# Eight PSUM banks in one ring and an earlier fourth product in the seven-product stage of a two-layer encoder

## The chip, the cores and the metric

One core of one Trainium2 chip. The metric is device time in microseconds (us) of one launch, as the median of several runs. The profile is one more execution, recorded instruction by instruction.

## The reference

Two layers, 1152 tokens (1024 of a prompt, 8 x 16 of a sample), model width 1024, feed-forward width 4096, all in float32:

```python
h = rms_norm(x, g1); q, k, v, a, b = split(h @ w_in)
x = x + concat([attention(q, k, v) * beta_a, conv(a * sigmoid(b)) * beta_c]) @ w_out
h = rms_norm(x, g2)
x = x + square(relu(h @ w_up)) @ w_down
```

The last line, the feed-forward, is what the change is about.

## The kernel before, in words

Tokens lie in three blocks of 384 (`BT`), transposed, so that x of a block is eight tiles of 128 x 384. Every float32 number is split into a high and a low part (`parted` for activations: a cast on ACT, L807, and a subtraction on DVE, L808; for weights a cast on ACT, L884, and a subtraction on POOL, L885), and a product of a 128x128 weight tile and a 128x384 activation tile is three matmuls (high by high, high by low, low by high).

The feed-forward of blocks 0 and 1 runs in part as a *stage of seven products*: block 0 and block 1, and four quarters of a weight block, are treated as a 2x2 by 2x2 block product and multiplied in seven products in place of eight. This stage takes the last half of the hidden columns, in four groups in each layer. A group is two *ups* (`pair_up`, j = 0 and 1, each seven products of 12 matmuls, L918) and one *down* (`pair_down`, two halves `mp`, each seven products into two banks of six matmuls, L992): 336 matmuls. `quad` loads the four quarters of a weight block by four DMAs (raw and A tiles); the call `sums()` inside it makes S1, S2, S3 (L871 on DVE, 128x512), and the product with S4 makes S4. An up leaves eight forms of the hidden activations (B11, T1, T2, B22, T3, B21, T4) as high and low parts in the tiles F; the down adds each finished bank to x (L995, DVE). In the down, `then` (a generator, `second()` in `run`) brings the third block's x back from memory (`kept`) and computes its RMSNorm, in pieces between products of the last group.

A compile-time scheduler sets the order on each engine from the code, the pools and its own estimate of durations; a tile that is allocated from a pool waits until the readers of the bank's last holder are done. PSUM has eight banks: three in pool `pp` (tag g, `pg()`) and five in `px` (tag x, `px_bank()`). Before, an up's three accumulators A, B, Z are three g banks, the five "less" and "plus" results stand in x banks, a down's four accumulators X and Z in x banks, and its product A12·B21 in a g bank for each half.

The RMSNorm lines named below: L235 and L247 are the small statistics (POOL, PE), L241 a PE sum over the squares (L260, ACT), L275 the product with the scale.

Of the kernel before, what the change touches and what calls it, by code (L numbers as in the profile page):

```python
# [10 lines left out]
AF = mybir.ActivationFunctionType  # L11
# [50 lines left out]
class Kernel:  # L62
# [628 lines left out]
    def hidden(self, ps):  # L691

        nc = self.nc
        hid = self.hp.tile([128, 2, BT], F32R, tag="hid", name=self.nm("hid"), bufs=4)
        f = self.tmp()
        nc.scalar.activation(f, ps, AF.Relu)  # L696
        nc.scalar.activation(f, f, AF.Square)
        nc.scalar.copy(hid[:, 0], f)  # L698
        nc.vector.tensor_tensor(out=hid[:, 1], in0=f, in1=hid[:, 0].bitcast(F32), op=ALU.subtract)  # L699
        return hid  # L700
# [204 lines left out]
            self.ahead = self.quad(src)  # L905
        return form, (lambda: self.ahead("sums")) if src is not None else (lambda: None)

    def pair_up(self, H, F):

        nc = self.nc  # L910
        form, sums = self.next_quad()
        A, B, Z = (self.pg()[0] for _ in range(3))

        def product(w, h, ps, start):
            u = form(w)
            for k in range(4):
                for i, (p, q) in enumerate(((0, 0), (0, 1), (1, 0))):
                    nc.tensor.matmul(ps, lhsT=u[:, p, k], rhs=H[h](q, k), start=start and k == 0 and i == 0, stop=k == 3 and i == 2, skip_group_check=True)  # L918

        def copy(ps):  # L920
            t = self.tmp()
            nc.scalar.copy(t, ps)
            return t

        def plus(o, t, ps):
            nc.vector.tensor_tensor(out=o, in0=t, in1=ps, op=ALU.add)
            return o

        def hidden(n, src, t):
            nc.scalar.activation(t, src, AF.Relu)  # L930
            nc.scalar.activation(t, t, AF.Square)
            return split(n, t)

        def split(n, t):
            self.parted(t, lambda p: F(n)[:, p])
            return t

        def less(n, x, y):
            t = self.px_bank()
            nc.vector.tensor_tensor(out=t, in0=x, in1=y, op=ALU.subtract)  # L940
            return split(n, t)

        product("A11", "B11", A, True)
        c1 = copy(A)
        product("S1", "T1", Z, True)
        z5 = copy(Z)
        product("S2", "T2", A, False)
        u2 = copy(A)
        product("S4", "B22", Z, False)
        b12 = plus(self.px_bank(), u2, Z)  # L950
        nc.scalar.activation(b12, b12, AF.Relu)
        nc.scalar.activation(b12, b12, AF.Square)
        product("S3", "T3", A, False)
        b22 = plus(z5, z5, A)
        b22 = hidden("B22", b22, b22)
        sums()
        product("A12", "B21", B, True)
        less("T3", b22, b12)
        b11 = plus(c1, c1, B)
        b11 = hidden("B11", b11, b11)  # L960
        product("A22", "T4", A, False)
        t1 = less("T1", b12, b11)
        t2 = less("T2", b22, t1)
        b21 = hidden("B21", A, self.tmp())
        less("T4", b21, t2)

    def px_bank(self):
        return self.px.tile([128, 512], F32, tag="x", name=self.nm("x"), bufs=5)[:, :BT]
# [8 lines left out]
    def pair_down(self, F, xs, between):  # L977

        nc = self.nc
        for mp in range(2):  # L980
            form, sums = self.next_quad()
            X, Z = ([self.px_bank() for _ in range(2)] for _ in range(2))
            for wn, hn, ps, start, b, half in (("A11", "B11", X, True, 0, 0), ("S1", "T1", Z, True, 1, 1), ("S2", "T2", X, False, 1, 0),
                                               ("S4", "B22", Z, False, 1, 0), ("S3", "T3", X, False, 1, 1), ("A12", "B21", None, True, 0, 0),
                                               ("A22", "T4", X, False, 0, 1)):
                u = form(wn)
                for i in range(2):
                    o = self.pg()[0] if ps is None else ps[i]
                    n = 0
                    for j in range(2):  # L990
                        for p, q in ((0, 0), (0, 1), (1, 0)):
                            nc.tensor.matmul(o, lhsT=u[:, p, 2 * i + j], rhs=F(j, hn)[:, q], start=start and n == 0, stop=n == 5, skip_group_check=True)  # L992
                            n += 1
                    m = 4 * half + 2 * mp + i
                    nc.vector.tensor_tensor(out=xs[b][:, m], in0=xs[b][:, m], in1=o, op=ALU.add)  # L995
                if wn == "S3":
                    sums()
                if between is not None:
                    next(between, None)

    def pair_feed(self, l, groups, xs, forms, then):
        for g in groups[::2]:
            F = self.hidden_forms()
            for j in range(2):
                self.pair_up(forms, lambda n, j=j: F(j, n))
            self.pair_down(F, xs, then if g == groups[-2] else None)

    def run(self):
        nc, tc, a = self.nc, self.tc, self.a
# [7 lines left out]
        x = [self.load_x(src[0])]  # L1017
# [3 lines left out]
        for l in range(DEPTH):  # L1021
            self.u, self.co, self.k, self.vb = [None] * NB, [None] * NB, [], []
            x, h, ao = [None] * NB, [None] * NB, [None] * NB
# [60 lines left out]
            forms, three, fourth = self.pair_forms(h[0], h[1])  # L1084
# [16 lines left out]
            def second(x=x, h=h, l=l):  # L1101
                x[2] = self.load_x(kept, self.mark)
                self.arena = [self.slot([4, 2, BT], F32, "f"), 0]
                for i, h[2] in enumerate(self.rmsnorm_steps(x[2], l, G2)):
                    for _ in range((5, 3, 1)[i]):
                        yield
                self.arena = None

# [1 line left out]
            self.aux = None  # L1110
            with pool(name=f"xp{l}", bufs=1) as self.xp, pool(name=f"px{l}", bufs=1, space=PS) as self.px:
                self.ahead("sums")
                then = second()
                self.pair_feed(l, range(pair, NG), x, forms, then)
                for _ in then:
                    pass
# [137 lines left out]
```

## Time and profile before

| | |
|---|---|
| median of 3 runs | 2439.61 us (2438.41 to 2440.89) |
| profiled execution | 2441.61 us, its span 2439.8 us |
| mean granted TensorE clock | 0.984 |
| PE busy | 2333.8 us (96%) |
| DVE, POOL, ACT busy | 1633.8 (67%), 1529.2 (63%), 1270.2 us (52%) |
| DMA | mean 109 GB/s |

PE is TensorE's matmuls, DVE VectorE, ACT ScalarE, POOL GpSimd. PE is busy nearly all the time, so the question of this kernel is where PE waits, and where it runs at a lower clock.

### The profile page before, as it was taken

What the parts mean: (1) busy time and instruction counts of PE and PEld (TensorE: products, weight loads), DVE (VectorE), ACT (ScalarE), POOL (GpSimd) and SP (SyncE); (2) the same over time, 40 slices, a digit from 0 to 9 for tenths busy, and PEclk for the clock granted to TensorE, in tenths of its full rate; (3) what the DMA queues carried; (4) which work ended last, traced back from release to release, by engine and by line L of the source; (5) the groups of instructions that cost most, each with busy time, mean ns of one, the idle gap of its engine ahead of it and who ended that gap; (6) DMA issues with size and microseconds to landing.
All of it is one profiled execution on the core that took longest, in us unless ns stands there. A gap on an engine that the chain in (4) does not pass through costs nothing.

```text
span 2439.8 us, 39000 instructions
## 1 busy us (share of the span) xinstructions
PE 2333.8 (96%) x13822; PEld 2268.8 (93%) x13822; DVE 1633.8 (67%) x2993; ACT 1270.2 (52%) x2732; POOL 1529.2 (63%) x1375
## 2 busy tenths in 40 slices
PE   6898899999998999999999999999999899999999
PEld 6888898989998998999999999999999899999999
DVE  4999986996376767687687764699834766752222
ACT  5467555654335555554566476466433554544442
POOL 6875575556466566776865776856445655666663
PEclk9999899999999999999999999999999999999999
DMA  5422433334322222444343344434333222245442
GB/s 177 138 90 91 120 104 109 111 102 134 113 91 70 70 70 70 163 122 129 103 121 107 118 155 131 130 98 126 96 106 102 61 65 70 83 146 148 126 128 75
DMA packets 164259, 266.49 MB, mean 109 GB/s; under 512 B 24752, under 2 KB 55728, under 8 KB 164016
## 3 DMA queue, kind: packets, MB, share of 16 engines
q1 hardware_dynamic: 164064, 264.01, 34.9%
q8 instruction: 108, 1.77, 0.3%
q14 instruction: 87, 0.71, 0.1%
HBM read 250.19 MB, written 16.05 MB: 109 GB/s over the span
## 4 chain that ended last, share of the span: by engine, by line
PE 75%; DVE 14%; POOL 3%; ACT 3%; issue 2%; DMA 1%; SPq 0%; DVEq 0%; POOLq 0%; ACTq 0%
PE g L715 13%; PE g L213 13%; PE g L215 13%; PE g L214 13%; PE x L992 8%; DVE c L347 5%; PE g L918 4%; PE m L715 2%; PE r L715 2%; POOL w L885 2%; PE c L715 1%; PE g L992 1%; PE s L525 1%; DMA A<-in_w 1%; PE m L560 1%
## 5 line engine op out<-in xcount | busy, mean ns | idle before, releaser
L206 POOL TENSOR_TENSOR w<-raw,w 128x512 fp32r<-128x512 f32 x728 | 967.0, 1338 | 587.4 <-ACT w L205 567.8
L205 ACT CAST w<-raw 128x512 fp32r<-128x512 f32 x728 | 445.9, 619 | 459.2 <-PE g L715 126.1
L213 PE MATMUL g<-h,w 128*128 128x384 f32 x1696 | 576.6, 341 | 8.4 <-ACT h L276 3.8
L215 PE MATMUL g<-h,w 128*128 128x384 f32 x1696 | 573.5, 338 | 0.0
L214 PE MATMUL g<-h,w 128*128 128x384 f32 x1696 | 573.2, 338 | 0.0
L347 DVE SCALAR_TENSOR_TENSOR c<-u,vec,c 128x384 f32<-128x384 f32 (+1 forms) x960 | 498.1, 519 | 19.0
L715 PE MATMUL g<-hid,w 128*128 128x384 f32 x2304 | 430.5, 340 | 10.7 <-DVE x L717 7.3
L715 PEld LDWEIGHTS g<-hid,w 128*128 128x128 f32 x2304 | 398.4, 188 | 19.7 <-DVE x L717 12.1
L213 PEld LDWEIGHTS g<-h,w 128*128 128x128 f32 x1696 | 320.9, 189 | 12.6 <-ACT h L276 4.6
L214 PEld LDWEIGHTS g<-h,w 128*128 128x128 f32 x1696 | 320.9, 189 | 1.1 <-DVE h L277 0.2
L215 PEld LDWEIGHTS g<-h,w 128*128 128x128 f32 x1696 | 320.8, 189 | 0.7
L699 DVE TENSOR_TENSOR hid<-t,hid 128x384 fp32r<-128x384 f32 x128 | 108.8, 850 | 192.3 <-ACT hid L698 192.1
L885 POOL TENSOR_TENSOR w<-S,w 128x512 fp32r<-128x512 f32 x96 | 134.3, 1405 | 155.6 <-ACT w L884 154.6
L992 PE MATMUL x<-F,w 128*128 128x384 f32 x960 | 188.3, 350 | 0.0
L717 DVE TENSOR_TENSOR x<-x,g 128x384 f32<-128x384 f32 x240 | 129.5, 548 | 77.4 <-PE g L715 76.9
L992 PEld LDWEIGHTS x<-F,w 128*128 128x128 f32 x960 | 179.6, 199 | 0.0
L995 DVE TENSOR_TENSOR x<-x,x 128x384 f32<-128x384 f32 x192 | 102.7, 549 | 83.5 <-PE x L992 83.4
L918 PE MATMUL g<-h,w 128*128 128x384 f32 x768 | 147.3, 338 | 11.7 <-ACT t L930 9.0
L918 PEld LDWEIGHTS g<-h,w 128*128 128x128 f32 x768 | 134.0, 188 | 16.3 <-ACT t L930 11.5
L696 ACT ACTIVATE t<-g 128x384 f32<-128x384 f32 x128 | 62.9, 492 | 141.0 <-PE g L215 140.0
L884 ACT CAST w<-S 128x512 fp32r<-128x512 f32 x96 | 59.7, 625 | 109.4 <-PE x L992 71.5
L885 POOL TENSOR_TENSOR w<-raw,w 128x512 fp32r<-128x512 f32 x64 | 84.1, 1315 | 46.0 <-ACT w L884 46.0
(213 smaller groups left out, 3786.7 us busy)
## 6 DMA issues: line engine op xcount, KB each, us to landing
raw<-in_w SPq DMA_DIRECT2D x792, 256.0 KB, 2.7
A<-in_w SPq DMA_DIRECT2D x64, 256.0 KB, 2.7
x<-in_x SPq DMA_DIRECT2D x24, 384.0 KB, 5.0
x<-xd SPq DMA_DIRECT2D x12, 384.0 KB, 5.4
kept<-x SPq DMA_DIRECT2D x4, 768.0 KB, 4.6
x<-kept SPq DMA_DIRECT2D x8, 384.0 KB, 4.1
xd<-x SPq DMA_DIRECT2D x4, 768.0 KB, 4.2
out_y<-x SPq DMA_DIRECT2D x4, 768.0 KB, 4.3
```

The source lines that it names most:

```text
L205: nc.scalar.copy(u[:, 0], raw)
L206: nc.gpsimd.tensor_tensor(out=u[:, 1], in0=raw, in1=u[:, 0].bitcast(F32), op=ALU.subtract)
L213: nc.tensor.matmul(ps, lhsT=u(0, k), rhs=h(0, k), start=k == 0, stop=False)
L214: nc.tensor.matmul(ps, lhsT=u(0, k), rhs=h(1, k), start=False, stop=False)
L215: self.pe = nc.tensor.matmul(ps, lhsT=u(1, k), rhs=h(0, k), start=False, stop=k == KT - 1)
L347: t = nc.vector.scalar_tensor_tensor(out=o, in0=src(k), scalar=w, in1=o, op0=ALU.mult, op1=ALU.add)
L699: nc.vector.tensor_tensor(out=hid[:, 1], in0=f, in1=hid[:, 0].bitcast(F32), op=ALU.subtract)
L715: self.pe = nc.tensor.matmul(ps, lhsT=u(p), rhs=hid[:, q], start=i == 0, stop=i == n - 1)
L717: nc.vector.tensor_tensor(out=x[:, m], in0=x[:, m], in1=ps, op=ALU.add)
L885: nc.gpsimd.tensor_tensor(out=u[:, 1], in0=f[n], in1=u[:, 0].bitcast(F32), op=ALU.subtract)
L918: nc.tensor.matmul(ps, lhsT=u[:, p, k], rhs=H[h](q, k), start=start and k == 0 and i == 0, stop=k == 3 and i == 2, skip_group_check=True)
L992: nc.tensor.matmul(o, lhsT=u[:, p, 2 * i + j], rhs=F(j, hn)[:, q], start=start and n == 0, stop=n == 5, skip_group_check=True)
```

## The change

All banks of the stage come from one ring, `bank8()`, of eight turns: five from `px`, three from `pg`. The seventh and eighth bank of an up are saved by forming T3 in the bank of b12 and T4 in that of t1. In the up, A12·B21 moves from sixth to fourth product, with b11 made behind it, and S4·B22 from fourth to sixth. In the down, A12·B21 takes its two banks (`Y`) from the ring. The third block's reload starts (`next(then)`) in the last up in place of the last down.

```diff
-    def pair_up(self, H, F):
+    def pair_up(self, H, F, then=None):
...
-        A, B, Z = (self.pg()[0] for _ in range(3))
+        A, Z, B = (self.bank8() for _ in range(3))
...
-        def less(n, x, y):
-            t = self.px_bank()
+        def less(t, x, y):
             nc.vector.tensor_tensor(out=t, in0=x, in1=y, op=ALU.subtract)
-            return split(n, t)
+            return t
...
         u2 = copy(A)
-        product("S4", "B22", Z, False)
-        b12 = plus(self.px_bank(), u2, Z)
-        nc.scalar.activation(b12, b12, AF.Relu)
-        nc.scalar.activation(b12, b12, AF.Square)
+        product("A12", "B21", B, True)
+        if then is not None:
+            next(then)
+        b11 = plus(c1, c1, B)
+        b11 = hidden("B11", b11, b11)
         product("S3", "T3", A, False)
         b22 = plus(z5, z5, A)
         b22 = hidden("B22", b22, b22)
         sums()
-        product("A12", "B21", B, True)
-        less("T3", b22, b12)
-        b11 = plus(c1, c1, B)
-        b11 = hidden("B11", b11, b11)
+        product("S4", "B22", Z, False)
+        b12 = plus(self.bank8(), u2, Z)
+        nc.scalar.activation(b12, b12, AF.Relu)
+        nc.scalar.activation(b12, b12, AF.Square)
         product("A22", "T4", A, False)
-        t1 = less("T1", b12, b11)
-        t2 = less("T2", b22, t1)
+        t1 = split("T1", less(self.bank8(), b12, b11))
+        t2 = split("T2", less(self.bank8(), b22, t1))
+        split("T3", less(b12, b22, b12))
         b21 = hidden("B21", A, self.tmp())
-        less("T4", b21, t2)
+        split("T4", less(t1, b21, t2))
+
+    def bank8(self):
+
+        self.turn = (self.turn + 1) % 8
+        return self.px_bank() if self.turn < 5 else self.pg()[0]
...
-            X, Z = ([self.px_bank() for _ in range(2)] for _ in range(2))
+            X, Z, Y = ([self.bank8() for _ in range(2)] for _ in range(3))
...
-                    o = self.pg()[0] if ps is None else ps[i]
+                    o = ps[i]
...
-                self.pair_up(forms, lambda n, j=j: F(j, n))
+                self.pair_up(forms, lambda n, j=j: F(j, n), then if j and g == groups[-2] else None)
...
-                    for _ in range((5, 3, 1)[i]):
+                    for _ in range((3, 3, 1)[i]):
```

The number of instructions on each engine stays what it was. In the rows that follow, g_ and x_ are PSUM banks, F_ tiles of hidden forms, T_ and h_ forms of the stage's input, w_ weight forms, S_, raw_ and A_ weight quarters and their sums, t_ temporaries, x_2764 and x_4025 the two blocks of x.

**The join, on PE** (second group of layer 0, between the last product of its second up and the first half of its down). Before:

```order
L992 MATMUL g_8934<-F_8491,w_8923 128x384 x3
L918 MATMUL g_8665<-T_7166,w_8788 128x384 x12
L992 MATMUL g_8926<-F_8491,w_8923 128x384
L992 MATMUL g_8934<-F_8491,w_8923 128x384
L992 MATMUL x_8828<-F_8489,w_8832 128x384 x6
L992 MATMUL x_8829<-F_8489,w_8832 128x384 x6
```

Now:

```order
L918 MATMUL g_8659<-T_7166,w_8778 128x384 x12
L998 MATMUL g_8822<-F_8485,w_8843 128x384
L998 MATMUL g_8821<-F_8486,w_8860 128x384 x3
L998 MATMUL g_8822<-F_8485,w_8843 128x384 x2
L998 MATMUL x_8820<-F_8485,w_8826 128x384 x6
L998 MATMUL x_8824<-F_8487,w_8917 128x384 x3
L998 MATMUL g_8821<-F_8486,w_8860 128x384
L998 MATMUL g_8823<-F_8485,w_8843 128x384 x6
L998 MATMUL g_8821<-F_8486,w_8860 128x384 x2
L998 MATMUL g_8822<-F_8486,w_8878 128x384 x6
L998 MATMUL x_8824<-F_8487,w_8917 128x384
L998 MATMUL x_8825<-F_8487,w_8917 128x384 x4
```

The L918 row with w_8788 (now w_8778) is A22·T4, after which B21's second half is formed. Before, the down's product with B21 (F_8491) followed at once; now 30 matmuls stand between, and B21's second half is first read by the single matmul into x_8824 (F_8487 holds T3 and B21). After these twelve rows comes the second half's first bank, x_8959, which takes over bank x_8797.

**The join, on DVE** (same place). Before:

```order
L940 TENSOR_TENSOR x_8807<-t_8700,x_8803 128x384
L871 TENSOR_TENSOR S_9057<-raw_8963,A_8965 128x512
L808 TENSOR_TENSOR F_8491<-t_8811,F_8491 128x384
L871 TENSOR_TENSOR S_9059<-S_9057,raw_8959 128x512
L871 TENSOR_TENSOR raw_8963<-raw_8959,raw_8963 128x512
L808 TENSOR_TENSOR F_8490<-x_8807,F_8490 128x384
L940 TENSOR_TENSOR x_8816<-t_8811,x_8807 128x384
L995 TENSOR_TENSOR x_2764<-x_2764,x_8828 128x384
```

Now:

```order
L808 TENSOR_TENSOR F_8486<-x_8797,F_8486 128x384
L871 TENSOR_TENSOR S_9051<-raw_8955,A_8957 128x512
L1001 TENSOR_TENSOR x_4025<-x_4025,g_8822 128x384
L808 TENSOR_TENSOR F_8487<-x_8774,F_8487 128x384
L871 TENSOR_TENSOR S_9053<-S_9051,raw_8951 128x512
L871 TENSOR_TENSOR raw_8955<-raw_8951,raw_8955 128x512
L939 TENSOR_TENSOR x_8793<-t_8804,x_8797 128x384
L1001 TENSOR_TENSOR x_2764<-x_2764,x_8820 128x384
L808 TENSOR_TENSOR F_8487<-t_8804,F_8487 128x384
```

The L939 row is T4's subtraction, the last reader of bank x_8797 (T2); before, T4's subtraction (x_8816) freed no bank that the down waited for. In both orders the three sums of the next weight block (L871) stand ahead of it.

**The start of the stage, on PE** (layer 0). Before:

```order
L715 MATMUL g_7848<-hid_7405,w_7574 128x384 x3
L715 MATMUL g_7848<-hid_7490,w_7584 128x384 x3
L918 MATMUL g_7893<-h_3248,w_7896 128x384
L918 MATMUL g_7893<-h_3249,w_7896 128x384
...
L918 MATMUL g_7893<-h_3248,w_7896 128x384
L918 MATMUL g_7895<-T_7164,w_7913 128x384 x2
```

Now:

```order
L918 MATMUL x_7893<-h_3249,w_7896 128x384
L715 MATMUL g_7840<-hid_7405,w_7574 128x384 x3
L715 MATMUL g_7840<-hid_7490,w_7584 128x384 x3
L715 MATMUL g_7848<-hid_7405,w_7574 128x384 x3
L715 MATMUL g_7848<-hid_7490,w_7584 128x384 x3
L918 MATMUL x_7893<-h_3248,w_7896 128x384
L918 MATMUL x_7894<-T_7164,w_7913 128x384 x2
```

A11·B11 (w_7896) stood behind the last products of the stage ahead (L715); now 11 of its 12 matmuls stand before the last two of these, and S1·T1 (w_7913) follows them after one matmul. In layer 1 the order here is as it was.

## Rows read from the trace of the kernel before

**Rows 1.** The chain that ended last: shares of the span by engine.

```profile
PE 75%; DVE 14%; POOL 3%; ACT 3%; issue 2%; DMA 1%; SPq 0%; DVEq 0%; POOLq 0%; ACTq 0%
```

**Rows 2.** Stretches: length, busy PE, PEld, DVE, ACT, POOL (instructions), clock, DMA share, GB/s.

```profile
722.20:990.00 267.80, 246.64 (x1348) 239.92 (x1347) 186.76 (x303) 135.24 (x266) 159.13 (x119) 0.97 0.23 71
1900.10:2171.80 271.70, 251.95 (x1375) 245.21 (x1375) 188.98 (x306) 136.75 (x269) 161.13 (x122) 0.97 0.24 74
...
2160.00:2200.00 40.00, 40.00 (x231) 40.00 (x231) 11.82 (x19) 20.07 (x36) 29.66 (x23) 1.00 0.68 218
```

**Rows 3.** Waits of PE, whole run: us in total, times, longest.

```profile
PE g L992 <- ACT F L807: 17.8, 8, 3.0
...
PE g L918 <- ACT t L930: 9.0, 8, 1.1
...
PE g L241 <- DVE f L265: 2.5, 2, 1.3
...
PE g L992 <- ACT hid L807: 2.1, 2, 1.7
PE g L992 <- POOL w L885: 2.0, 2, 1.1
PE g L247 <- POOL s L235: 2.0, 2, 1.1
...
PE g L992 <- DVE x L926: 0.8, 2, 0.4
```

**Rows 4.** PE's timeline at a join: start, length, what, [idle before <-releaser].

```profile
824.26 2.35 PE L918 MATMUL g<-T,w 128*128 128x384 f32 x12
829.04 0.61 PE L992 MATMUL g<-F,w 128*128 128x384 f32 x2 [2.43 <-ACT F L807]
```

**Rows 5.** ACT's timeline at the same join.

```profile
826.65 0.49 ACT L930 ACTIVATE t<-g 128x384 f32<-128x384 f32 x1 [0.21 <-PE g L918]
...
828.48 0.51 ACT L807 CAST F<-t 128x384 fp32r<-128x384 f32 x1
```

**Rows 6.** Stretches after waits: one at full clock, the first of seven slow.

```profile
829.00:836.00 7.00, 6.96 (x40) 6.96 (x41) 7.00 (x13) 2.72 (x5) 3.37 (x4) 1.00 0.13 40
...
763.60:769.40 5.80, 5.80 (x20) 5.80 (x20) 5.35 (x11) 1.58 (x3) 0.64 (x1) 0.51 0.13 47
...
sum 31.20, PE 29.17 PEld 28.16 DVE 29.88 ACT 8.15 POOL 5.61; mean PE 4.17 PEld 4.02 DVE 4.27 ACT 1.16 POOL 0.80
```

**Rows 7.** DVE's timeline at the start of the stage, layer 0.

```profile
722.38 0.55 DVE L717 TENSOR_TENSOR x<-x,g 128x384 f32<-128x384 f32 x1 [0.48 <-PE g L715]
722.85 0.68 DVE L871 TENSOR_TENSOR S<-raw,A 128x512 f32<-128x512 f32 x1
...
724.78 1.77 DVE L871 TENSOR_TENSOR S<-raw,A 128x512 f32<-128x512 f32 x1
```

**Rows 8.** POOL at the same place, its timeline.

```profile
725.96 1.75 POOL L885 TENSOR_TENSOR w<-A,w 128x512 fp32r<-128x512 f32 x1
```

**Rows 9.** DVE's sums from 722 to 2172 by form, and DVE's waits there.

```profile
L871 DVE TENSOR_TENSOR S<-raw,A 128x512 f32<-128x512 f32 x32 | 30.6, 956 | 21.8 <-DMA A<-in_w 19.5 <-POOL w L885 1.7 <-issue 0.4
...
DVE S L871 <- DMA A<-in_w: 19.5, 15, 5.0
```

**Rows 10.** ACT in the last group of layer 0, its timeline.

```profile
951.69 0.85 ACT L260 ACTIVATE f<-x 128x768 f32<-128x768 f32 x1 [0.35 <-DMA x<-kept]
```

**Rows 11.** PE's timeline at the last product of an up.

```profile
886.57 0.69 PE L992 MATMUL g<-F,w 128*128 128x384 f32 x3
887.38 2.35 PE L918 MATMUL g<-T,w 128*128 128x384 f32 x12
```

**Rows 12.** The page's group of POOL's splits, and PE waiting for one at 726.

```profile
L885 POOL TENSOR_TENSOR w<-raw,w 128x512 fp32r<-128x512 f32 x64 | 84.1, 1315 | 46.0 <-ACT w L884 46.0
...
726.05 2.38 PE L918 MATMUL g<-T,w 128*128 128x384 f32 x12 [0.62 <-POOL w L885]
```

**Rows 13.** DVE where the third block's RMSNorm ends, its timeline.

```profile
960.35 4.29 DVE L275 SCALAR_TENSOR_TENSOR f<-x,vec,g 128x384 f32<-128x384 f32 x8 [0.21 <-PE g L247]
```

More of the change, by code (lines that the diff above doesn't have):

```diff
@@ L981, in pair_down @@
             form, sums = self.next_quad()
-            X, Z = ([self.px_bank() for _ in range(2)] for _ in range(2))
+            X, Z, Y = ([self.bank8() for _ in range(2)] for _ in range(3))
             for wn, hn, ps, start, b, half in (("A11", "B11", X, True, 0, 0), ("S1", "T1", Z, True, 1, 1), ("S2", "T2", X, False, 1, 0),
-                                               ("S4", "B22", Z, False, 1, 0), ("S3", "T3", X, False, 1, 1), ("A12", "B21", None, True, 0, 0),
+                                               ("S4", "B22", Z, False, 1, 0), ("S3", "T3", X, False, 1, 1), ("A12", "B21", Y, True, 0, 0),
                                                ("A22", "T4", X, False, 0, 1)):
@@ L1112, in run @@
                 self.ahead("sums")
+                self.turn = 7
                 then = second()
```

## The prediction

> **What bounds the kernel now.** I began with the chain that ended last: PE holds 75% of it and DVE 14% [rows 1], so time is won where PE waits or runs slowly. Next came the windows of the two stages that the change touches. They last 267.8 and 271.7 us, 539.5 together, and hold 1348 + 1375 = 2723 matmuls [rows 2]. A stretch without waits has 231 in 40 us [rows 2], 0.1732 us each. At that rate the stages would take 471.6 us; 68 are lost.
>
> The list of PE's waits shows where. The longest group is the *join*, where the first half of a down meets the end of its second up: PE waits for the cast of B21's second half (`L992 <- ACT F L807`), 17.8 us in eight waits, one in each of the eight groups; then 9.0 us in eight waits of the second up for the first up's last product to be read, since both use the same g bank [rows 3]. In the timeline 12 matmuls of A22·T4 start at 824.26 and are fed by 824.26 + 12 x 0.173 = 826.34; the next starts at 829.04 [rows 4]. That is 2.70 us where the list says 2.43, so a wait costs some 0.27 more than its idle time. ACT shows why: the relu starts at 826.65, and after a square the cast starts at 828.48 [rows 5].
>
> [...]
>
> **What the change removes.**
> (i) The wait for the first up's A, 9.0 us in eight: the second up's fourth product now has a ring bank that was free long before.
> (ii) The join's waits for B21 and its kin: 17.8 in eight, `ACT hid` 2.1 in two, `DVE x L926` 0.8 in two [rows 3]. The order now puts 30 matmuls, 5.2 us, between A22·T4 and the first use of B21's second half. The path to it takes 829.04 - 826.34 = 2.7 us [rows 4, 5]; 2.5 are to spare.
> (iii) `L241 <- DVE f` 2.5 and `L247 <- POOL s` 2.0, four waits in the reload's RMSNorm [rows 3]: by the new order some 50 matmuls, 8.7 us, stand between L241 and L247, and no wait was longer than 1.3.
> (iv) `L992 <- POOL w` 2.0 in two: same join, same cover [rows 3].
> Together 9.0 + 20.7 + 4.5 + 2.0 = 36.2 us in 26 waits; with 26 x 0.27 = 7.0 it is 43.2. Nearly all the falls of the clock stood behind these waits, so I give back 13 of the 15 us: 56.2. Bounds for that: 0 if waits as long as before return elsewhere, 15.
>
> **What it adds.** None of the following is a wait that the trace has at that place, so each is bounded by rows.
> *n1, start of layer 0.* S1 is summed on DVE behind the last x adds, which follow the last L715 products; 11 matmuls of A11·B11 that stood behind these as cover now stand before them. What is uncovered is at least that sum, 0.68 [rows 7], and at most the cover that went, 11 x 0.173 = 1.9; a cast follows the sum, so I take 1.9, once.
> *n2, the first ups.* POOL must make four splits while PE does 22 to 24 matmuls (3.8 to 4.2 us). A split takes 1.315 in the mean, four 5.3 [rows 12]: 1.0 late, twice. PE waited 0.62 for one here before [rows 12]. And b22's sum stands behind three L871 sums, 0.68 each alone and 1.77 at worst [rows 7]; 1.8 twice. Sum 5.6, bounds 2 and 8.
> *n3, last product of the first up.* It now follows S3·T3's partner after one matmul in place of three. Before, it came at 887.38 where three matmuls from 886.57 would end at 887.09: 0.29 late [rows 11]. Two matmuls less are 0.35 more: 0.65 in six ups, 3.9 (0 to 6).
> *n4.* The second up's A22·T4 behind b22: 0.3 in eight, 2.4 (0 to 0.8 each).
> *n5, the new critical handover.* The second half's first bank of a down now takes over T2's bank, whose last reader is T4's subtraction. On DVE's queue, behind A22·T4, stand five small operations (0.55 each [rows 7]) and three sums L871, T4's subtraction last. PE has 35 matmuls meanwhile, 6.1 us. With sums at 0.68 DVE needs 5 x 0.55 + 3 x 0.68 = 4.8 and PE waits for nothing; with 1.77, 8.1, and PE waits 2.0; their mean is 956 ns [rows 9], which makes 5.6, just inside. The first sum also needs its weights' DMA: DVE waited for that 19.5 us in 15 places, 1.3 each [rows 9], which would bring 3.1. Between 0 and 3.1 I take 1.2 a group, half of the 2.0 and most of a restart; eight groups, 9.6.
> *n6, last group.* The reload is one up earlier, so four squares of 0.85 us, of which one waited for its DMA before [rows 10], stand on ACT ahead of B11's cast: 1.7 twice, 3.4 (0 to 6).
> *n7, end of the stage.* The eight L275 operations take 4.29 us [rows 13], against 24 matmuls, 4.2: 0.5 twice, 1.0.
> Together 1.9 + 5.6 + 3.9 + 2.4 + 9.6 + 3.4 + 1.0 = 27.8.
> The diff's remaining edits cost nothing: as many instructions as before on every engine, and the in-place subtractions read PSUM and write PSUM as they did.
>
> [...] The 0.68 and the 1.77 of L871 are the same operation [rows 7]; the long one ran beside a POOL split, which itself took 1.75 [rows 8] against a mean of 1.315 [rows 12]. [...]
>
> **Sum.** 56.2 - 27.8 = 28.4 us less. The profiled execution is 2441.6, so 2413.2 of that kind; the median lies 2.0 lower: 2411.
>
> **Rivals.**
> A, the forecast: 2402 to 2424. Chance 0.55.
> B, the new waits close by themselves, since the scheduler spread the matmuls and most bounds reach 0: with 13 of the 27.8 left the gain is 43.2, the time 2396; with all at their low bounds (1 + 2 + 1) some 2388. For it: the mean sums fit in n5's cover. Against: n2's splits don't fit. 0.13.
> C, DVE's sums stay beside POOL splits in every group. At 1.77 n5 is 2.0 + 0.27 a group, 18.2 (8.6 more), n2 is 8 (2.4 more), n4 6.4 (4 more), and waits of over 2 us take half of the clock's return, 6.5: 28.4 - 21.5 = 7, so 2433; without the clock's part 2426. For it: POOL is busy 159 of 268 us [rows 2], so more than half of the sums start beside a split if nothing orders them. Against: the mean of 956 ns, which is nearer to 0.68 than to 1.77 [rows 7, 9]. 0.17.
> [...]
> D, the change does nothing that shows: PE's waits move from B21 to T4 and from one bank to another with their sum kept, and the time is within 5 us of 2440. For it: PE is 92% busy in the stages [rows 2] and DVE's work there is unchanged. 0.06.
> E, slower, by one mechanism: the first sum, S1, waits for its weights at the join. Its longest wait was 5.0 [rows 9]. It then holds T3's split, two more sums and T4's subtraction, which before the change freed no bank. DVE needs 4.8 + 5.0 = 9.8, PE waits 3.7 in each group, 29.6 (20 more than n5), and the clock falls as it did behind waits of 2.43 to 3.0 [rows 3], so its 13 don't come back: 28.4 - 33 = -4.6, which is 2444. It decides from (28.4 - 13 + 9.6) / 8 = 3.1 us a group. Against it: the mean of these waits is 1.3 and they stood in 15 of 32 places [rows 9]. 0.09.
>
> **How the numbers follow.** A measurement of this kernel tells about 0.2%, 4.9 us, from no change. Faster are A, B and C, 0.85; same is D, 0.06; slower E, 0.09. The range holds A, the upper half of B and nearly all of C: 2395 to 2433, about 0.8.
>
> **What would show it.** In the profile of the changed kernel the rows `PE <- ACT F L807` and `<- ACT t L930` are gone or below 0.5 us each (i, ii). A wait of PE at the down's first bank for the subtraction L939 or the cast behind it, around 1 us in each group, shows n5; none there shows B, 2 us C, over 3 E. The two stages together take 511 us in place of 539.5. The granted clock over the run goes from 0.984 to 0.99 or more; if it stays, 13 us of my sum are wrong. At the start of layer 0 a wait of 1 to 2 us for the cast of S1 shows n1, and waits for POOL splits there n2. The mean of L871 should stay near 956 ns; if it rises over 1.3 us, C holds. I would be wrong altogether if the time went outside the stages: the order there is the same, and their windows should last as before.

## The result and the profile after

The changed kernel takes 2413.28 us in the median of four runs (2407.56 to 2418.6), beside 2439.3 for the kernel before: a ratio of 0.9892, interval 0.9869 to 0.9915. The forecast was 2411. Its profiled execution is the fastest of the four, 2407.56 us with a span of 2405.8; a second profile of the same kernel (first experiment) has 2413.4 and 2411.6, nearer to the median.

The windows of the changed kernel between the same matmuls of PE (to 0.2 us) as 718.0 to 1000.0 and 1890.0 to 2175.0 before (columns as in [rows 2]):

```profile
714.94:981.90 266.96, 254.82 (x1430) 247.60 (x1430) 203.86 (x313) 143.04 (x279) 168.97 (x128) 1.00 0.27 87
1871.90:2140.90 269.00, 258.28 (x1446) 250.48 (x1445) 210.52 (x328) 141.64 (x278) 172.53 (x129) 1.00 0.25 81
sum 535.96, PE 513.10 PEld 498.07 DVE 414.39 ACT 284.69 POOL 341.51; mean PE 256.55 PEld 249.04 DVE 207.19 ACT 142.34 POOL 170.75
```

The two stretches took 282.0 + 285.0 = 567 us before: 31 us are saved, 15 in layer 0 and 16 in layer 1, and the granted clock is 1.00 in both. The other 3 us of the profiled difference lie ahead of the stages, where the first of these windows already starts 3.1 us earlier with the same order of instructions on PE: from 366.6 to 373.3 the granted clock was 0.50 in the profile before, and here it was 1.00. With the order there unchanged, these 3 us are not put down to the change. Between the stages and behind them the starts of the same matmuls moved by 0.1 us.

Waits of PE in the changed kernel (us in total, times, longest; L998, L1001, L939 are L992, L995, L940 of before):

```profile
PE x L918 <- POOL w L885: 4.6, 6, 1.1
PE x L918 <- DVE t L926: 4.5, 6, 1.3
...
PE x L918 <- ACT w L884: 2.9, 3, 1.7
PE x L998 <- DVE x L1001: 2.4, 4, 1.0
...
PE g L918 <- DVE t L926: 1.6, 2, 0.8
PE g L998 <- ACT F L807: 1.4, 4, 0.4
...
PE g L998 <- DVE F L808: 1.0, 3, 0.4
...
PE x L998 <- DVE x L939: 1.0, 1, 1.0
...
PE g L998 <- DVE f L275: 0.8, 2, 0.4
...
PE g L998 <- DVE x L939: 0.7, 3, 0.2
```

All rows of [rows 3] are gone but the cast L807, now 1.4 us in four. None of the new waits reaches 2 us. The join at which [rows 4] shows 2.43 us now reads, on PE and on DVE:

```profile
819.54 1.22 PE L998 MATMUL g<-F,w 128*128 128x384 f32 x6
820.60 1.73 PE L998 MATMUL x<-F,w 128*128 128x384 f32 x9
822.17 2.77 PE L998 MATMUL g<-F,w 128*128 128x384 f32 x15
824.77 1.04 PE L998 MATMUL x<-F,w 128*128 128x384 f32 x5
826.77 2.54 PE L998 MATMUL x<-F,w 128*128 128x384 f32 x13 [0.95 <-DVE x L939]
```

```profile
821.63 1.02 DVE L871 TENSOR_TENSOR S<-raw,A 128x512 f32<-128x512 f32 x1 [1.22 <-DMA A<-in_w]
...
824.46 1.78 DVE L871 TENSOR_TENSOR raw<-raw,raw 128x512 f32<-128x512 f32 x1
826.17 0.55 DVE L939 TENSOR_TENSOR x<-t,x 128x384 f32<-128x384 f32 x1
```

This is n5 as forecast: 35 matmuls run without a gap, then PE waits for T4's subtraction, which stands behind a late load and three sums. It comes at this length in one group of the eight, though: L939 is waited for in four groups, and in the other three for 0.25 us or less.

### The profile page after: what moved, and what is told of

It reads as the page before. It is cut to its first block, busy times and chain, and to the rows that moved or that the text cites. A ratio compares the mean times of both kernels' runs of the same rounds, so it can differ in the third digit from the quotient of the medians.

```text
span 2405.8 us, 38983 instructions
## 1 busy us (share of the span) xinstructions
PE 2319.9 (96%) x13822; PEld 2254.8 (94%) x13822; DVE 1658.2 (69%) x2993; ACT 1270.5 (53%) x2732; POOL 1530.3 (64%) x1375
## 3 DMA queue, kind: packets, MB, share of 16 engines
q1 hardware_dynamic: 164064, 264.01, 35.5%
q8 instruction: 108, 1.77, 0.3%
## 4 chain that ended last, share of the span: by engine, by line
PE 76%; DVE 16%; POOL 3%; issue 2%; DMA 2%; ACT 2%; SPq 0%; DVEq 0%; POOLq 0%; ACTq 0%
PE g L715 14%; PE g L213 13%; PE g L215 13%; PE g L214 13%; DVE c L347 5%; PE x L998 4%; PE x L918 4%; PE g L998 3%; PE g L918 2%; PE m L715 2%; PE r L715 2%; POOL w L885 1%; PE c L715 1%; DMA A<-in_w 1%; PE s L525 1%
## 5 line engine op out<-in xcount | busy, mean ns | idle before, releaser
L213 PE MATMUL g<-h,w 128*128 128x384 f32 x1696 | 576.4, 340 | 7.2 <-ACT h L276 3.8
L214 PE MATMUL g<-h,w 128*128 128x384 f32 x1696 | 573.1, 338 | 1.1 <-DVE h L277 1.1
L215 PE MATMUL g<-h,w 128*128 128x384 f32 x1696 | 573.4, 338 | 0.0
L715 PE MATMUL g<-hid,w 128*128 128x384 f32 x2304 | 431.2, 341 | 9.3 <-DVE x L717 6.3
L715 PEld LDWEIGHTS g<-hid,w 128*128 128x128 f32 x2304 | 399.6, 189 | 17.8 <-DVE x L717 10.8
L213 PEld LDWEIGHTS g<-h,w 128*128 128x128 f32 x1696 | 320.8, 189 | 11.4 <-ACT h L276 4.6
L214 PEld LDWEIGHTS g<-h,w 128*128 128x128 f32 x1696 | 320.6, 189 | 2.8 <-DVE h L277 2.0
L215 PEld LDWEIGHTS g<-h,w 128*128 128x128 f32 x1696 | 320.4, 189 | 0.7
L885 POOL TENSOR_TENSOR w<-S,w 128x512 fp32r<-128x512 f32 x96 | 138.5, 1446 | 120.0 <-ACT w L884 119.7
L998 PE MATMUL x<-F,w 128*128 128x384 f32 x624 | 119.2, 336 | 3.4 <-DVE x L1001 2.4
L885 POOL TENSOR_TENSOR w<-raw,w 128x512 fp32r<-128x512 f32 x64 | 90.6, 1416 | 41.0 <-ACT w L884 39.7
L998 PEld LDWEIGHTS x<-F,w 128*128 128x128 f32 x624 | 109.4, 188 | 4.9 <-DVE x L1001 2.5
L998 PE MATMUL g<-F,w 128*128 128x384 f32 x528 | 108.3, 340 | 4.1 <-ACT F L807 1.4
L884 ACT CAST w<-S 128x512 fp32r<-128x512 f32 x96 | 59.7, 622 | 96.1 <-DVE S L871 51.1
L998 PEld LDWEIGHTS g<-F,w 128*128 128x128 f32 x528 | 92.6, 188 | 8.4 <-ACT F L807 2.7
L885 POOL TENSOR_TENSOR w<-A,w 128x512 fp32r<-128x512 f32 x64 | 87.0, 1364 | 18.6 <-ACT w L884 18.4
```

What stands on the lines that cost most here:

```text
L213: nc.tensor.matmul(ps, lhsT=u(0, k), rhs=h(0, k), start=k == 0, stop=False)
L214: nc.tensor.matmul(ps, lhsT=u(0, k), rhs=h(1, k), start=False, stop=False)
L215: self.pe = nc.tensor.matmul(ps, lhsT=u(1, k), rhs=h(0, k), start=False, stop=k == KT - 1)
L715: self.pe = nc.tensor.matmul(ps, lhsT=u(p), rhs=hid[:, q], start=i == 0, stop=i == n - 1)
L885: nc.gpsimd.tensor_tensor(out=u[:, 1], in0=f[n], in1=u[:, 0].bitcast(F32), op=ALU.subtract)
```

## Experiments

Ratios are to the kernel before, timed on the same chip in the same series.

**The same kernel again.** No edit.

> The changed kernel as it is, for its spread and as the neighbour of the next three. Its four times lay between 2407.6 and 2418.6 us. Theory (the gain sits in the two stages): the stages last 31 us less than before, within 2 us of the first profile, and the median is 2411 to 2416. Rival (the profiled execution was a lucky one, its stages are shorter than usual): the stages last 25 to 28 us less, with a wait that the first profile did not show, or with a stretch at the lower clock.

2413.68 us (2409.63 to 2415.06), 0.9877 (0.9864 to 0.9890). Its stages take 266.83 + 272.41 us, 27.7 less than before, where the first profile had 31: the rival holds, the first was a good execution. Nearly all of the difference lies in one join of layer 1. The timeline of it in the first profile (DVE, POOL, PE), then in the second, and the window of the second behind its wait:

```profile
1967.12 0.69 DVE L871 TENSOR_TENSOR S<-raw,A 128x512 f32<-128x512 f32 x1 [0.54 <-DMA A<-in_w]
...
1967.33 1.64 POOL L885 TENSOR_TENSOR w<-S,w 128x512 fp32r<-128x512 f32 x1 [0.80 <-ACT w L884]
...
1972.68 0.80 PE L998 MATMUL g<-F,w 128*128 128x384 f32 x3 [0.23 <-DVE x L939]
```

```profile
1969.49 1.63 DVE L871 TENSOR_TENSOR S<-raw,A 128x512 f32<-128x512 f32 x1 [0.96 <-DMA A<-in_w]
...
1969.27 1.30 POOL L885 TENSOR_TENSOR w<-S,w 128x512 fp32r<-128x512 f32 x1 [0.80 <-ACT w L884]
...
1976.31 0.90 PE L998 MATMUL g<-F,w 128*128 128x384 f32 x3 [1.92 <-DVE x L939]
```

```profile
1976.30:1980.30 4.00, 3.99 (x14) 4.00 (x15) 2.63 (x4) 2.78 (x6) 1.28 (x1) 0.57 0.17 66
```

The load came 0.42 us later (0.96 for 0.54). In the first profile the sum starts 0.21 us ahead of a POOL split, takes 0.69, and the split 1.64; in the second it starts 0.22 behind the split and takes 1.63, the split 1.30. So in each profile the one of the two that started second was the long one: the sum took 0.94 us more than when it came first, the split 0.34 more. PE's wait grows from 0.23 to 1.92 us: 0.42 of it is the load, 0.94 this sum, and 0.32 the subtraction L808 behind it, which took 1.51 for 1.19. Behind the wait the clock falls to 0.57 over the 4.0 us shown, 1.7 us more. So less than half a microsecond of a transfer stands at the head of the 3.4 us by which the two stages of layer 1 differ (272.41 and 269.00).

**The product order alone.** The kernel before with the two products exchanged; the steps that read each product move with it, and T3's subtraction moves behind T2's:

```diff
-        product("S4", "B22", Z, False)
+        product("A12", "B21", B, True)
...
-        product("A12", "B21", B, True)
+        product("S4", "B22", Z, False)
...
-        less("T3", b22, b12)
...
+        less("T3", b22, b12)
```

> The kernel before, with A12·B21 as fourth and S4·B22 as sixth product of an up and nothing else: banks, reload and in-place subtractions as before. Theory (order and ring each close the join and the second up's wait alone, because each puts matmuls behind A22·T4): 18 matmuls now stand between A22·T4 and the need for B21's second half, 3.1 us against a path of 2.7, so the waits for L807 and L930 go, the clock comes back, and 7 to 12 us of waits at the start and for b22's sum come with the order: 2400 to 2415 us. Rival (only eight banks in one ring close them): the two waits stay at 20 us or more, 2425 to 2440.

**The ring alone.** The changed kernel with that exchange and the reload undone.

> The changed kernel with the products in the order of before and the reload where it was: the ring and the in-place T3 and T4 alone. Theory (each alone is enough): 21 matmuls, 3.6 us, stand between A22·T4 and the need for B21's second half, and the fourth and sixth products have banks of their own, so both waits go; the waits of A22·T4 for b22's sum (6 us in the changed kernel) do not come, as A12·B21 stands between: 2395 to 2412. Rival (the moved product is what closes the second up's wait and the join): 2425 to 2440.

Order alone: 2428.32 us, 0.9944 (0.9932 to 0.9956). Ring alone: 2432.81, 0.9952 (0.9939 to 0.9965). PE's longest waits, order alone first:

```profile
PE g L918 <- DVE t L926: 14.1, 10, 2.1
PE x L992 <- DVE F L808: 5.8, 5, 1.4
PE g L918 <- ACT t L930: 4.4, 4, 1.5
PE g L241 <- DVE f L265: 2.3, 1, 2.3
```

```profile
PE g L996 <- DVE x L939: 12.1, 6, 4.2
PE g L996 <- ACT t L930: 7.3, 8, 2.7
```

Both times lie where the rivals had them, but neither theory nor rival has the reason. Each part removes the long wait for B21's cast and opens others: the order alone leaves A22·T4 right behind b22's sum (L926) and half of the second up's bank waits (L930); the ring alone puts the down behind T4's subtraction (L939, up to 4.2 us) and lets the clock fall in its stages, 0.97 and 0.98. By the ratios they are worth some 14 and 12 us, and the two together (the same kernel again, same series) some 30. The stages of the profiled executions are 15.3 and 14.7 us shorter than before, but the ring's was one of its two fastest of six (2427.5; the other four took 2432.2 to 2433.9). The lists of waits show why the parts add up to about the whole: L926 goes from 14.1 to 6.1 us where the ring comes to the order, L939 from 12.1 to 1.7 and L930 from 7.3 to nothing where the order comes to the ring.

**The reload where it was.** The changed kernel without the `then` of `pair_up`, and with (5, 3, 1).

> The changed kernel with the third block's reload where it was (started in the last down). Theory (the earlier reload takes away 5.6 us of waits in the RMSNorm and brings back 6 elsewhere: casts behind squares, L275 and L277 at the end): within 3 us of the changed kernel. Rival (the reload's place is a gain of its own): 5 us or more slower than the changed kernel, with the waits for L265 and L235 back.

2408.87 us, 0.9859 (0.9845 to 0.9873), not to be told from the changed kernel beside it (0.9877). Its PE has no wait for L265 or L235 in the stages. So those 4.5 us of [rows 3] went with the ring, and not with the reload's new place: between the last matmul of L241 and the first of L247 in layer 0 stand 2 others before, 39 in the ring alone and 46 here, both with the old place. The order alone still has 2.3.

**Filling the join.** The kernel before, in `pair_down`:

```diff
+                    if ps is None and mp == 0 and i == 0:
+                        for d in range(9):
+                            nc.tensor.matmul(o, lhsT=u[:, 0, 0], rhs=F(1, "T1")[:, 0], start=True, stop=True, skip_group_check=True)
```

> The kernel before, with nine extra matmuls in each group, right behind A22·T4 of the second up, from T1's form into the bank of A12·B21, which that product then overwrites: they compute nothing that is kept and fill part of the join's wait. Theory (the lower clock behind the joins costs 13 us of its own): the wait for B21 stays, now split into idle time of about 1.2 us and 1.6 us of matmuls, the granted clock stays at full behind it, and the time falls by 8 to 13 us, to 2430 to 2435 beside 2443. Rival (the clock falls for another reason, or the fill delays the products): within 4 us of the kernel before, or slower.

2442.37 us, 1.0005 (0.9992 to 1.0019). That is the rival's time, but it hides two effects. The extra matmuls wait for T1's cast themselves (`PE g L991 <- ACT F L807: 14.5, 8, 4.3` in its list of waits). In the second and third group of each layer that wait is 0.95 us in place of 2.43, the join behind it is filled, and the granted clock stays at 1.00 in all four. In the first and last groups PE waits longer than that, and the clock falls in four stretches, 23.8 us in all (the mean granted clock of this profile is 0.987, beside 0.984 in the profile before); waits for L926 (5.4 us) and L922 (3.8) are new. Windows from one wait for L930 to the next hold one join each. The two of layer 0 before, then the second of them with the fill:

```profile
814.44:877.56 63.12, 59.45 (x336) 58.49 (x337) 43.20 (x72) 32.26 (x65) 37.82 (x28) 1.00 0.22 68
877.56:942.19 64.63, 60.96 (x336) 60.01 (x336) 45.46 (x74) 32.32 (x65) 38.29 (x28) 0.97 0.21 65
```

```profile
875.97:939.67 63.70, 60.98 (x345) 60.03 (x345) 45.13 (x73) 32.08 (x65) 37.28 (x28) 1.00 0.23 66
```

The two windows before have the same wait of 2.43 us at the join (829.04 and 892.16); only behind the second the clock fell, to 0.52 from 892.6 to 895.7. So one such fall cost 1.5 us by itself. The fill wins 0.9 us where the clock fell before and loses 0.6 where it did not (63.69). For the stage as a whole the clock's part stays with the windows: 31.2 us at granted clocks of 0.50 to 0.53 before [rows 6], none in the stages of the first profile (1.00 in both).

**T4 in T2's bank.** In the changed kernel, in the ring alone, and with the old reload:

```diff
-        split("T4", less(t1, b21, t2))
+        split("T4", less(t2, b21, t2))
```

> The changed kernel with T4 formed in T2's bank in place of T1's. T1's bank, which the down's second half takes first, is then free before T4's subtraction, and T2's bank is needed 16 matmuls later. Theory (n5: PE waits there for T4's subtraction behind three sums, and a long such wait drops the clock): the waits for L939 at L998, 2.6 to 5.5 us by two profiles, go, and the spread of the times narrows: 3 to 7 us less than the changed kernel, 2406 to 2411 beside its 2413.7. Rival (the handover only moves on to the next bank): within 2 us of it, with waits as long for T4's cast or L1001.

> The ring alone (products and reload as before) with T4 formed in T2's bank. Theory (the ring alone falls short since its down waits for T4's subtraction, 12.1 us in six waits up to 4.2, and the clock falls behind them, some 11 us): both go, 2405 to 2415 us, as good as the changed kernel without its moved product. Rival (the moved product is needed to cover the join): the waits for the relu L930 (7.3 us) and others grow to fill the place, over 2420.

> The changed kernel with T4 formed in T2's bank and the reload where it was before. Theory (the two edits touch different waits, and the reload's place is worth nothing or costs up to 5 us): 2401 to 2411 us. Rival (the old place of the reload brings its RMSNorm's waits back): slower than the kernel with T4 in T2's bank by 3 us or more.

2421.09 us, 0.9915 (0.9901 to 0.9928); 2438.04, 0.9986 (0.9978 to 0.9995); 2419.74, 0.9915 (0.9900 to 0.9929). All three are slower than without the edit. The waits for L939 are gone, as the theory said, but others are longer; in the ring alone L922 takes 10.7 us, L930 9.1 and a subtraction (`DVE hid L808`) 8.4, as its rival had it. PE's waits in the first of them, and ACT at one:

```profile
PE x L918 <- ACT t L922: 9.5, 6, 1.8
PE g L998 <- ACT F L807: 5.9, 8, 1.0
PE g L918 <- ACT t L922: 4.7, 7, 1.4
```

```profile
798.68 0.53 ACT L930 ACTIVATE t<-t 128x384 f32<-128x384 f32 x1 [2.94 <-DVE t L926]
799.24 0.52 ACT L931 ACTIVATE t<-t 128x384 f32<-128x384 f32 x1
799.79 0.51 ACT L807 CAST F<-t 128x384 fp32r<-128x384 f32 x1
800.21 0.47 ACT L922 COPY t<-x 128x384 f32<-128x384 f32 x1
```

A bank freed earlier changed the order that the scheduler wrote: in the first ups of the later groups A12·B21 now stands ahead of S2·T2, and on ACT b11's relu ahead of u2's copy. The relu waits 2.94 us for a sum on DVE; the copy, which PE needs, waits behind it. PE at this place:

```profile
795.75 1.38 PE L918 MATMUL x<-T,w 128*128 128x384 f32 x7
796.96 2.27 PE L918 MATMUL x<-h,w 128*128 128x384 f32 x12
800.74 2.54 PE L918 MATMUL x<-h,w 128*128 128x384 f32 x13 [1.50 <-ACT t L922]
```

S2·T2, which the copy reads, ended by 797.1, while ACT was idle. Ahead of the relu the copy (0.47 us) would have been done before the 12 matmuls behind S2·T2 were, at 799.2, and PE would not have waited here.

**Two other hand-outs of the same banks.** In the changed kernel, first

```diff
-            X, Z, Y = ([self.bank8() for _ in range(2)] for _ in range(3))
+            Z, X, Y = ([self.bank8() for _ in range(2)] for _ in range(3))
```

> The changed kernel with the down's banks asked from the ring as Z, X, Y in place of X, Z, Y; nothing else. By the built order the products of the ups stand as in the changed kernel, and 38 matmuls in place of 35 stand at the join ahead of the second half's first bank. Theory (n5 is priced by the cover there): its waits for L939 get shorter by up to 0.5 us each, and 0 to 4 us are won: 2409 to 2414 beside the changed kernel's 2413.7. Rival (any other handing out of banks makes the scheduler write another order, which costs more than it wins, as T4 in T2's bank did): 2418 or more.

> Z, X, Y as in the run above, and the reload where it was before. The kernel with the old reload was 4.8 us below the changed one, with intervals that touch. Theory (the reload's new place is worth nothing): within 3 us of the Z, X, Y kernel. Rival (the old place is better by some 5 us): 4 us or more below it, 2403 to 2408.

and then

```diff
+        o2, o1 = self.bank8(), self.bank8()
-        t1 = split("T1", less(self.bank8(), b12, b11))
-        t2 = split("T2", less(self.bank8(), b22, t1))
+        t1 = split("T1", less(o1, b12, b11))
+        t2 = split("T2", less(o2, b22, t1))
```

> The changed kernel with T2's bank asked before T1's; nothing else. By the built order A12·B21 stands ahead of S2·T2 in the first ups, as with T4 in T2's bank, but u2's copy stands ahead of b11's relu on ACT, as in the changed kernel; and A22·T4 of a first up stands 24 matmuls later. Theory (T4 in T2's bank lost 16 us because ACT held u2's copy behind a relu that waits for DVE): these waits for L922 stay under 6 us, the first ups' waits for L926 go, 2406 to 2416. Rival (A12·B21 ahead of S2·T2 is what costs): 2419 or more, with waits for L922 of 10 us or more.

> T2's bank asked before T1's, and the reload where it was before. Theory (the reload's place is worth nothing, the waits behind it only change their names): within 4 us of the kernel with T2's bank first, whose ratio to the kernel before is 0.986, so 0.984 to 0.988. Rival (the reload's old place is better by 5 us): 0.984 or less, with the waits for L277 gone and no new ones for L265 and L235.

Z first: 2416.99 us, 0.9897 (0.9881 to 0.9914), between the theory's range and the rival's, with the old reload 2412.08, 0.9871 (0.9855 to 0.9886). With Z first the stages are 35.5 us shorter than before, 263.61 + 267.86 us, and L939's waits gone from the list, as the longer cover has it; but behind the stage of layer 0 the new order loses 8 us (by the starts of the same matmuls), at a clock of 0.91 in this window of it:

```profile
974.00:1010.00 36.00, 31.37 (x171) 30.43 (x170) 19.13 (x28) 18.02 (x32) 23.66 (x23) 0.91 0.57 192
```

T2 first: 2408.79, 0.9860 (0.9843 to 0.9878), with the old reload 2405.24, 0.9852 (0.9833 to 0.9870), the lowest of all. PE's longest waits with T2 first:

```profile
PE g L918 <- ACT t L922: 6.2, 2, 3.2
PE x L918 <- ACT w L884: 2.9, 3, 1.7
PE x L918 <- POOL w L885: 2.9, 4, 1.1
```

L922 is waited for in two places only, for u2's copy stands ahead of the relu on ACT, and these 6.2 us are just over the 6 that the theory allowed. This fits the explanation of the runs before by ACT's order. It does not rule out PE's: by the trace only 5 of the 12 matmuls of A12·B21 stand ahead of S2·T2 here, where with T4 in T2's bank all 12 did. The waits for L926 fell to 1.3 us.

Four pairs of kernels now differ in the reload's place alone. With the old place the ratio is lower by 0.0018, 0, 0.0026 and 0.0008, with intervals that overlap each time. So no pair shows that the earlier reload wins anything; whether it costs some 3 us (the mean of the four) is open.

## Why the prediction held, point by point

The forecast was 28.4 us in the profiled execution and about as much in the median; the stages gave 31.0 and 27.7 in two profiles, and the median 26.0.

**(i), (ii) and (iv) right**, 31.7 us of waits removed, as worked out from the matmuls that stand between; the 1.4 us of L807 that the changed kernel has are counted under n6. What the prediction did not see is that ring and order each close the wait for B21's cast alone, and that each alone opens others; so either gives about half.

**(iii) right in size, and not by the reload's move:** with the old place the waits are gone too.

**The clock** came back whole in the first profile: its two stages have 1.00. No run shows the forecast's 15 us as such. What the profile before shows is seven stretches, 31.2 us in all [rows 6], at granted clocks of 0.50 to 0.53; these two have the highest and the lowest (columns as in [rows 2]):

```profile
2005.30:2008.50 3.20, 3.20 (x12) 3.20 (x12) 3.15 (x7) 0.00 (x0) 0.00 (x0) 0.53 0.27 82
...
2134.80:2141.20 6.40, 5.32 (x18) 4.82 (x18) 6.10 (x13) 3.05 (x5) 2.53 (x6) 0.50 0.12 39
```

The 15 us are an estimate from them, 31.2 x 0.49, for the 13 taken. In the second profile one stretch fell, to 0.57 over 4.0 us. The 0.27 us that a wait costs beyond its idle time was too much, read from one place. In the join above, five matmuls from 824.77 are fed by 824.77 + 5 x 0.173 = 825.64; the next starts at 826.77, 1.13 later for 0.95 of idle time, so 0.18, and the mean over all waits of the stages is 0.17 before and after. Over 26 waits that is 2.3 us less given back.

**The new waits**, by idle time. n1: 1.72, for the 1.9 (`723.12`, below). n2: the start's waits for L885 (4.6), L884 (2.9 - 1.7) and, twice 1.3, L926 are 8.4, where before the same lines had 4.0 (2.8 for L884, 1.2 for L885): 4.4 more, for the 5.6. n3 and n4: 6.1 of L926 without these 2.6, 3.5 for the 6.3. n5: 1.7 for L939 and 2.4 for the x additions L1001 of the same queue, 4.1 for the 9.6 (6.6 in the second profile, where L939 has 4.4); this is the term that was mis-sized, since DVE was late in some groups only. Its upper bound of 3.1 a group should have been 3.3 (2.0 and 1.3). n6: 2.4 for the 3.4. n7: 0.8 for L275 and 1.1 for L277, 1.9 for the 1.0. The n1 row, on PE:

```profile
723.12 0.62 PE L918 MATMUL x<-T,w 128*128 128x384 f32 x2 [1.72 <-ACT w L884]
```

These terms, n1 to n7, make 18 us of idle time, and some 5 more for thirty restarts at 0.18: 23 for the 27.8. Put together, 36.2 of idle time, 4.7 of restarts and 15 of clock, less 23, make 33 us where the first profile's stages gave 31.0; the last 2 us are not explained. So the mechanism was right. That the median came within 2.3 us of the forecast is partly luck: the new waits were priced 5 us too high, the restarts 2.3 too high, the clock 2 too low, and one execution differs from the next by more than that.

**Rival C** is half true. The third sum slowed from 887 to 1565 ns in the mean, and the other two hardly, to 1042 and 1026 from 956 [rows 9] and 988:

```profile
L871 DVE TENSOR_TENSOR raw<-raw,raw 128x512 f32<-128x512 f32 x32 | 50.1, 1565 | 0.0
L871 DVE TENSOR_TENSOR S<-raw,A 128x512 f32<-128x512 f32 x32 | 33.3, 1042 | 19.8 <-DMA A<-in_w 18.7 <-POOL w L885 1.0
L871 DVE TENSOR_TENSOR S<-S,raw 128x512 f32<-128x512 f32 x32 | 32.8, 1026 | 0.5
```

At these means the queue ahead of T4's subtraction takes 5 x 0.55 + 1.56 + 1.04 + 1.03 = 6.4 us, just over the 6.1 of cover. Of the 32 third sums 26 took more than 1.6 us (6 before), and each of these began while a POOL split was running; the six that began beside none took 0.68. The mean of the three sums is 1.21 us, under the 1.3 at which the prediction would have given C the case. The split that the prediction sets beside the sum of 1.77 us (724.78, [rows 7]) is not the one that ran when the sum began: the split of 725.96 [rows 8] began 1.18 us after it, and another had been running for 0.45 us:

```profile
724.33 1.67 POOL L885 TENSOR_TENSOR w<-S,w 128x512 fp32r<-128x512 f32 x1 [8.84 <-ACT w L884]
```

**Rival E**'s mechanism, the late load, is there, and it is what set two executions of the same kernel 3 us apart at the join above; that it makes the rest of the 11 us between the four times is not shown. In neither profile of the changed kernel did the wait reach 3.1 us; in the ring alone it did (4.2). E took falls of the clock to come behind waits of 2.43 to 3.0 us; that fits five of the seven before. The other two stood behind two waits of 0.98 to 1.30 us each, close together at the end of a stage (957.45 and 2134.46).

## What to carry to other kernels

Count the matmuls that the new order leaves between a producer's last input and its first use, and set them against the chain's length: that told which waits would go. Price a handover by the whole queue ahead of it on its engine, with the late load and the slow operations in it: here 6.4 us of DVE work at the mean times beside 6.1 of cover, with a load that DVE waited 0.54 or 0.96 us for at one join and a sum that took 0.69 or 1.63. With cover and chain that close, 0.42 us of a DMA stood at the head of 3.4 us between two executions. And where a scheduler writes the order, every change of a bank is a change of order: of four ways to hand out the same eight banks here the times lay between 2408.8 and 2421.1 us, so the neighbours of a good one are worth a run.

## What was not expected

Two halves of a change that each give 12 to 15 us and together about 30, though each alone already closes the same wait. One sum of 128x512 that took 0.69 us where it started 0.21 us ahead of a POOL operation and 1.63 where it started 0.22 us behind one, and a fall of the clock (0.57 over 4.0 us) behind a wait of 1.92 us, where a wait of 2.43 (829.04, [rows 6]) did not bring one.
